# Layer 1 of a two-layer decoder: its wide products cut into 256-column products, with other places in SBUF and other orders

## Chip, cores and metric

One core of one Trainium2 chip. The metric is the device time of one execution in microseconds (us): 2316.28 us before the change, the median of two runs (2315.99 and 2316.57). A product here is one matmul instruction of TensorE: 128 rows of weights that stand still, and a number of columns that stream past them.

## What is computed

A decoder of two layers over 272 tokens (16 meta tokens and 256 of the input), model width 2048, 16 heads of 128, MLP width 8192, all in float32. Layer 0 (forgetting attention) computes all 272 tokens; layer 1 (stick-breaking attention) needs queries, output projection and MLP for the last 256 alone. Cut to what matters:

```
for layer in range(2):
    a = rms_norm(h, norm_attn[layer])
    if layer == 0:
        q, k, v, f = split(a @ fox_w_in)
        h = h + forgetting_attention(q, k, v, cumsum(log_sigmoid(f + b))) @ fox_w_o
    else:
        k, v = split(rms_norm(h, kv_norm) @ w_kv)
        h = h + stick_breaking_attention(a @ sb_w_q, k, v) @ sb_w_o
    h = h + square(relu(rms_norm(h, norm_mlp[layer]) @ w_up[layer])) @ w_down[layer]
return rms_norm(h, final_norm)[16:]
```

## The kernel before

Activations stay in SBUF with features on the partitions: `hT` holds 16 chunks of 128 features by 272 tokens. Every wide matrix product runs in `gemm_group` (L183): one call computes 512 output features, as four accumulators (`m` = 0 to 3, one PSUM bank each) that sum over 16 chunks of 128 inputs, in four blocks `kb` of four chunks `kc`. The groups are numbered `u` in program order: 1 to 12 are query, key and value of layer 0, 13 to 16 its output projection, 17 to 48 its MLP (for each quarter `f` of the width four up groups and four down groups), 49 to 52 the queries of layer 1, 53 to 60 its shared keys and values (which need all 272 tokens), 61 to 64 its output projection, and 65 to 96 its MLP in the same way.

To keep accuracy, each float32 operand is split into a high part, rounded to the fast float32r format, and a low part, the rest. Weights arrive by DMA on SP's queue in halves of a block (`raw`, 512 KB, L207), ScalarE writes `whi` (L218) and VectorE `wlo` (L219); four buffers of each let this run ahead. The activations ("rows" in the code, class `Split`, L118) hold high and low part of a chunk in 640 columns, at the column offsets in `ROWS` (L27). Three of the four partial products are added up: whi·hi, whi·lo and wlo·hi.

In layer 0 (and for keys and values) these are three products of 272 columns per chunk and accumulator. In layer 1 (`pairs=True`) hi and lo, 304 columns apart, are read as one operand of 2 x 256 columns:

```
gemm_matmul(accs[m], whi, sp.both[:, 4 * kb + kc], ...)       # 512 columns
gemm_matmul(accs[m][:, :n], wlo, sp.hi[:, 4 * kb + kc], ...)  # 256 columns
```

So whi·hi + wlo·hi stands in the left half of the bank and whi·lo in the right half, and VectorE (and ScalarE) add the halves when the bank is emptied: `total` (L259) for queries and up groups, two additions in `residual_add` (L255) for output projection and down groups. The very last chunk (group 96, `m` = 3, `apart`) runs as three products of 256 columns in one half. In layer 1 `wlo` is stored 16 columns further right than in layer 0.

The order of TensorE's instructions within and across groups is pinned as written (`gemm_matmul`, L175); other work, such as attention and norms, is placed between by a scheduler. A product's weights are loaded by an instruction of its own in the profile (LDWEIGHTS, engine PEld).

Of the kernel before, what the change touches and what calls it, by code (L numbers as in the profile page):

```python
# [12 lines left out]
ALU = mybir.AluOpType  # L13
AX = mybir.AxisListType

P = 128
D = 2048
NC = D // P
M = 16
# [7 lines left out]
ROWS = {0: (48, 368), M: (0, 304)}  # L27
# [6 lines left out]
def yoco_kernel(ctx: ExitStack, tc: tile.TileContext, hT_in, gains, b_f, w_f, w_qkv0, w_o0, w_up, w_dn,  # L34
# [83 lines left out]
    class Split:  # L118


        def __init__(self, label, t0):
# [3 lines left out]
            hi, lo = ROWS[t0]  # L125
# [3 lines left out]

            self.both = rows[:, :, :2 * d].rearrange("p c (i t) -> p c i t", i=2)[:, :, :, :n]  # L130
# [52 lines left out]
    def gemm_group(wblk, sp, t0, evac, before={}, after={}, load_x=None, pairs=False, apart=()):  # L183


# [7 lines left out]
        for kb in range(4):  # L193
# [31 lines left out]

            if load_x is not None and kb == 0:
                runs = [([kc], range(4)) for kc in range(4)]
            elif kb in (0, 3):
                runs = [(range(4), [m]) for m in range(4)]
            else:  # L230
                runs = [(range(2 * hf, 2 * hf + 2), range(4)) for hf in range(2)]
            pinned[0] = load_x is None
            for kcs, ms in runs:
                paired = [m for m in ms if pairs and m not in apart]
                single = [m for m in ms if m not in paired]
                for kc in kcs:
                    for m in paired:
                        gemm_matmul(accs[m], parts[kc // 2][0][:, kc % 2, m * P:(m + 1) * P], sp.both[:, 4 * kb + kc],
                                    start=kb == kc == 0, stop=False)
                for kc in kcs:  # L240
                    for m in paired:
                        gemm_matmul(accs[m][:, :n], parts[kc // 2][1][:, kc % 2, m * P:(m + 1) * P],
                                    sp.hi[:, 4 * kb + kc], start=False, stop=kb == kc == 3)
                for m in single:
                    for kc in kcs:
                        wh, wl = (w[:, kc % 2, m * P:(m + 1) * P] for w in parts[kc // 2])
                        hi, lo = sp.hi[:, 4 * kb + kc], sp.lo[:, 4 * kb + kc]
                        gemm_matmul(accs[m][:, :n], wh, hi, start=kb == kc == 0, stop=False)
                        gemm_matmul(accs[m][:, :n], wh, lo, start=False, stop=False)
                        gemm_matmul(accs[m][:, :n], wl, hi, start=False, stop=kb == kc == 3)  # L250
# [488 lines left out]
```

## Time and profile before

| | |
|---|---|
| median of the runs | 2316.28 us |
| profiled execution | 2316.17 us |
| its span, first to last instruction | 2314.5 us |
| granted TensorE clock, mean | 0.998 |
| HBM read | 407.29 MB, 177 GB/s over the span |
| mean busy share of VectorE, ScalarE | 58%, 46% |

"PE" is TensorE computing, "PEld" its weight loads, DVE VectorE, ACT ScalarE, POOL GpSimd, SP SyncE. A product's recorded duration (some 276 ns for 256 columns) is longer than the step from one start to the next, because products overlap in the array; the time a stretch takes comes from the starts, or from a stretch's length and its count of instructions. In the timeline a row merges neighbouring instructions of one kind: start, time covered, engine, line, operation, tiles, shape and count. In the grouped rows stand the busy time and the mean duration in ns, then the idle time ahead of them.

### The profile page before, as it was taken

To read this page: it belongs to the slowest core of one execution; us is meant where nothing else is said; L and a number is where in the kernel's file an instruction comes from. 1 tells how busy PE (TensorE), PEld (TensorE's weight loads), DVE (VectorE), ACT (ScalarE), POOL (GpSimd) and SP (SyncE) were. 2 spreads that over 40 slices of the span, in tenths; PEclk is the share of its full clock that TensorE was granted. 3 is DMA by queue.
4 is the path that set the end of the run, shared out by engine and by line. 5 is a ranking of instruction groups with operands and counts; after the bars stand their busy time and mean duration, and the time that the engine had idled before them with its cause. 6 is when DMAs were issued, how large, how long until landed. Compare 5 with 4: busy or idle time off the path is not lost.

```text
span 2314.5 us, 39954 instructions
## 1 busy us (share of the span) xinstructions
PE 2303.4 (100%) x16486; PEld 2183.1 (94%) x16486; DVE 1350.1 (58%) x1923; ACT 1064.1 (46%) x1477; POOL 40.8 (2%) x58
## 2 busy tenths in 40 slices
PE   9999999999999999999999999999999999999998
PEld 9999999999999999999998999988888888888887
DVE  7665555655454455445566555566665665665665
ACT  6434344543344344344445444455543543543553
POOL 1000000000000000000000000000000000000000
PEclk9999999999999999999999999999999999999999
DMA  6545445455555555555555444455556556556563
GB/s 233 169 155 170 166 163 170 168 187 174 181 170 186 179 175 181 173 184 175 182 178 200 157 146 146 146 169 196 193 188 199 185 190 200 185 191 199 183 200 128
DMA packets 116630, 412.00 MB, mean 178 GB/s; under 512 B 13264, under 2 KB 16736, under 8 KB 116448
## 3 DMA queue, kind: packets, MB, share of 16 engines
q1 hardware_dynamic: 114560, 406.29, 52.7%
q10 hardware_dynamic: 1888, 3.16, 0.4%
q8 instruction: 129, 2.11, 0.4%
q14 instruction: 53, 0.43, 0.1%
HBM read 407.29 MB, written 2.11 MB: 177 GB/s over the span
## 4 chain that ended last, share of the span: by engine, by line
PE 99%; DVE 0%; DMA 0%; ACT 0%; issue 0%; SPq 0%; DVEq 0%; ACTq 0%
PE acc L177 96%; PE ps L407 0%; PE pza L586 0%; PE pv L340 0%; PE po L469 0%; PE po L625 0%; PE pzb L587 0%; PE po L626 0%; PE po L470 0%; DMA g_sb<-gains 0%; PE po L627 0%; DVE ob L681 0%; PE pf L306 0%; PE pf L307 0%; PE pta L601 0%; PE pta L602 0%
## 5 line engine op out<-in xcount | busy, mean ns | idle before, releaser
L219 DVE TENSOR_TENSOR wlo<-raw,whi 128x1024 fp32r<-128x1024 f32 (+1 forms) x773 | 931.6, 1217 | 741.8 <-ACT whi L218 740.6
L218 ACT ACTIVATE whi<-raw 128x1024 fp32r<-128x1024 f32 (+1 forms) x773 | 799.1, 1050 | 948.0 <-PE acc L177 873.8
L177 PE MATMUL acc<-x_u,whi 128*128 128x272 f32 (+2 forms) x3088 | 647.9, 321 | 0.0
L177 PE MATMUL acc<-x_m,whi 128*128 128x272 f32 (+1 forms) x3072 | 646.2, 322 | 0.0
L177 PEld LDWEIGHTS acc<-x_u,whi 128*128 128x128 f32 x3088 | 499.5, 188 | 26.6
L177 PEld LDWEIGHTS acc<-x_m,whi 128*128 128x128 f32 x3072 | 497.5, 188 | 27.2
L177 PE MATMUL acc<-x_u,wlo 128*128 128x272 f32 (+1 forms) x2048 | 443.3, 281 | 0.0
L177 PE MATMUL acc<-x_m,wlo 128*128 128x272 f32 (+1 forms) x2048 | 441.0, 281 | 0.0
L177 PE MATMUL acc<-x_a,whi 128*128 128x272 f32 (+1 forms) x1792 | 360.6, 306 | 0.1
L177 PEld LDWEIGHTS acc<-x_u,wlo 128*128 128x128 f32 x2048 | 338.4, 188 | 15.8
L177 PEld LDWEIGHTS acc<-x_m,wlo 128*128 128x128 f32 x2048 | 337.5, 188 | 15.9
L177 PEld LDWEIGHTS acc<-x_a,whi 128*128 128x128 f32 x1792 | 284.2, 188 | 9.4 <-issue 0.7
L177 PE MATMUL acc<-x_a,wlo 128*128 128x272 f32 (+1 forms) x1024 | 254.0, 286 | 0.0
L177 PE MATMUL acc<-x_kv,whi 128*128 128x272 f32 x1024 | 194.1, 288 | 0.0
L177 PEld LDWEIGHTS acc<-x_a,wlo 128*128 128x128 f32 x1024 | 179.1, 188 | 5.3 <-DVE wlo L219 0.6
L177 PE MATMUL acc<-x_o,whi 128*128 128x272 f32 (+1 forms) x768 | 162.4, 322 | 0.0
L177 PEld LDWEIGHTS acc<-x_kv,whi 128*128 128x128 f32 x1024 | 160.6, 188 | 0.4
L177 PE MATMUL acc<-x_kv,wlo 128*128 128x272 f32 x512 | 147.3, 288 | 0.0
L257 DVE TENSOR_TENSOR hT<-acc,hT 128x256 f32<-128x256 f32 (+1 forms) x239 | 102.4, 428 | 70.5 <-PE acc L177 68.8
L177 PEld LDWEIGHTS acc<-x_o,whi 128*128 128x128 f32 x768 | 124.3, 188 | 6.7
L177 PE MATMUL acc<-x_o,wlo 128*128 128x272 f32 (+1 forms) x512 | 111.0, 282 | 0.0
L177 PEld LDWEIGHTS acc<-x_kv,wlo 128*128 128x128 f32 x512 | 96.5, 188 | 0.1
(226 smaller groups left out, 1040.0 us busy)
## 6 DMA issues: line engine op xcount, KB each, us to landing
raw<-w_up SPq DMA_DIRECT2D x256, 512.0 KB, 4.7
raw<-w_dn SPq DMA_DIRECT2D x256, 512.0 KB, 4.8
raw<-w_qkv SPq DMA_DIRECT2D x92, 512.0 KB, 4.3
raw<-w_o SPq DMA_DIRECT2D x64, 512.0 KB, 4.4
raw<-w_kv SPq DMA_DIRECT2D x64, 512.0 KB, 3.9
raw<-w_q SPq DMA_DIRECT2D x32, 512.0 KB, 4.8
fk<-f_dram ACTq DMA_DIRECT2D x4, 544.0 KB, 5.1
raw<-w_qkv SPq DMA_DIRECT2D x7, 256.0 KB, 4.6
```

What stands on the lines that cost most here:

```text
L177: ins = nc.tensor.matmul(*args, **kw).ins
L218: on_act = nc.scalar.activation(hp, src, AF.Copy)
L219: on_dve = nc.vector.tensor_tensor(out=lp, in0=src, in1=hp.bitcast(F32), op=ALU.subtract)
L257: nc.vector.tensor_tensor(out=hT[:, c, t0:], in0=a, in1=hT[:, c, t0:], op=ALU.add)
```

## The change

Layer 1 drops the 512-column products. `pairs`, `apart`, `Split.both` and `total` go; all groups issue three products per chunk and accumulator, in layer 1 of 256 columns each and all into the same accumulator columns. Emptying it takes one instruction less (two less in queries and up groups).

The places are now given by stage. `ROWS` is keyed by the rows' name, and low parts lie 320 columns after high parts everywhere; `columns_of_weights` shifts `whi` and `wlo` alike:

| layer-1 groups | rows start at column | weights start at column |
|---|---|---|
| queries 49-52, up 65-68, 73-76, 81-84, 89-92 | 0 | 16 |
| output projection 61-64 | 48 | 0 |
| down 69-72 | 48 | 0 |
| down 77-80 | 16 | 32 |
| down 85-88 | 48 | 32 |
| down 93-96 | 32 | 48 |

All other groups keep rows at 48 and weights at 0, and layer 0 keeps its order of products. A column is four bytes.

By group, `order` gives one of three nestings of products (chunk kc, accumulator m, pair), and in every fourth group the blocks `kb` 1 and 2 run as one stretch of four chunks:

```
+ROWS = {"a0": (48, 368), "kv": (48, 368), "o0": (48, 368), "m0": (48, 368), "u0_0": (48, 368),
+        "u0_1": (48, 368), "u0_2": (48, 368), "u0_3": (48, 368),
+        "a1": (0, 320), "o1": (48, 368), "m1": (0, 320), "u1_0": (48, 368), "u1_1": (16, 336),
+        "u1_2": (48, 368), "u1_3": (32, 352)}
+def columns_of_weights(u):
+    if u < 49 or 53 <= u <= 64:
+        return 0
+    f, g = divmod(u - 65, 8)
+    return 16 if u < 53 or g < 4 else (0, 32, 32, 48)[f]
+def order(u, kcs, ms, pairs):
+    way = (u - 1) % 4
+    if way == 0 or way == 3:
+        return [(kc, m, *pair) for pair in pairs for kc in kcs for m in ms]
+    if way == 1:
+        return ([(kc, m, *pair) for kc in kcs for m in ms for pair in pairs[:2]] +
+                [(kc, m, *pairs[2]) for kc in kcs for m in ms])
+    return [(kc, m, *pair) for kc in kcs for m in ms for pair in pairs]
...
-                whi, wlo = whi[:, :, :512], wlo[:, :, 16:528] if pairs else wlo[:, :, :512]
+                o = columns_of_weights(u)
+                whi, wlo = whi[:, :, o:o + 512], wlo[:, :, o:o + 512]
...
+            elif t0 and u % 4 == 0 and kb in (1, 2):
+                runs = [(range(4), range(4))]
...
             for kcs, ms in runs:
-                paired = [m for m in ms if pairs and m not in apart]
...
+                pairs = ((0, sp.hi), (0, sp.lo), (1, sp.hi))
+                if t0:
+                    products = order(u, kcs, ms, pairs)
+                else:
+                    products = [(kc, m, *pair) for m in ms for kc in kcs for pair in pairs]
+                left = {m: 3 * len(kcs) for m in ms}
+                for kc, m, part, x in products:
+                    first, left[m] = kb == kc == 0 and left[m] == 3 * len(kcs), left[m] - 1
+                    gemm_matmul(accs[m][:, :n], parts[kc // 2][part][:, kc % 2, m * P:(m + 1) * P], x[:, 4 * kb + kc],
+                                start=first, stop=kb == kc == 3 and left[m] == 0)
...
     def residual_add(c, acc, t0):
-        for a in acc:
-            nc.vector.tensor_tensor(out=hT[:, c, t0:], in0=a, in1=hT[:, c, t0:], op=ALU.add)
...
-        nc.scalar.copy(to, acc[1])
-        nc.vector.tensor_tensor(out=to, in0=acc[0], in1=to, op=ALU.add)
...
+        nc.vector.tensor_tensor(out=hT[:, c, t0:], in0=acc, in1=hT[:, c, t0:], op=ALU.add)
```

How instructions move on TensorE: the first half of block 1 in group 70 (a down group of layer 1; `x_u1_0` are its rows, `whi_70_1_0` the high weights of group 70, block 1, half 0). Before:

```order
L177 MATMUL acc_70_0_18477<-x_u1_0_17427,whi_70_1_0_18529 128x512
L177 MATMUL acc_70_1_18478<-x_u1_0_17427,whi_70_1_0_18529 128x512
L177 MATMUL acc_70_2_18479<-x_u1_0_17427,whi_70_1_0_18529 128x512
L177 MATMUL acc_70_3_18480<-x_u1_0_17427,whi_70_1_0_18529 128x512
...
L177 MATMUL acc_70_0_18477<-x_u1_0_17427,wlo_70_1_0_18530 128x256
L177 MATMUL acc_70_1_18478<-x_u1_0_17427,wlo_70_1_0_18530 128x256
L177 MATMUL acc_70_2_18479<-x_u1_0_17427,wlo_70_1_0_18530 128x256
L177 MATMUL acc_70_3_18480<-x_u1_0_17427,wlo_70_1_0_18530 128x256
```

and now:

```order
L198 MATMUL acc_70_0_19225<-x_u1_0_17891,whi_70_1_0_19293 128x256 x2
L198 MATMUL acc_70_1_19226<-x_u1_0_17891,whi_70_1_0_19293 128x256 x2
L198 MATMUL acc_70_2_19227<-x_u1_0_17891,whi_70_1_0_19293 128x256 x2
L198 MATMUL acc_70_3_19228<-x_u1_0_17891,whi_70_1_0_19293 128x256 x2
...
L198 MATMUL acc_70_0_19225<-x_u1_0_17891,wlo_70_1_0_19294 128x256
L198 MATMUL acc_70_1_19226<-x_u1_0_17891,wlo_70_1_0_19294 128x256
L198 MATMUL acc_70_2_19227<-x_u1_0_17891,wlo_70_1_0_19294 128x256
L198 MATMUL acc_70_3_19228<-x_u1_0_17891,wlo_70_1_0_19294 128x256
```

Each 512-column product has become two of 256 columns with the same weights, each with a weight load of its own. In group 71, the next, the same place reads:

```order
L198 MATMUL acc_71_0_19473<-x_u1_0_17891,whi_71_1_0_19541 128x256 x2
L198 MATMUL acc_71_0_19473<-x_u1_0_17891,wlo_71_1_0_19542 128x256
L198 MATMUL acc_71_1_19474<-x_u1_0_17891,whi_71_1_0_19541 128x256 x2
L198 MATMUL acc_71_1_19474<-x_u1_0_17891,wlo_71_1_0_19542 128x256
L198 MATMUL acc_71_2_19475<-x_u1_0_17891,whi_71_1_0_19541 128x256 x2
L198 MATMUL acc_71_2_19475<-x_u1_0_17891,wlo_71_1_0_19542 128x256
```

Here the three products of one accumulator and chunk follow one another, as in layer 0. On VectorE, emptying the up group 68 (`relu_1_0_12` is output chunk 12 of layer 1's first quarter) before:

```order
L264 TENSOR_TENSOR relu_1_0_12_18233<-acc_68_0_18077,relu_1_0_12_18233 128x256
L501 SCALAR_TENSOR_TENSOR relu_1_0_12_18233<-relu_1_0_12_18233,rstd_m1_17525 128x256
L264 TENSOR_TENSOR relu_1_0_13_18249<-acc_68_1_18078,relu_1_0_13_18249 128x256
L501 SCALAR_TENSOR_TENSOR relu_1_0_13_18249<-relu_1_0_13_18249,rstd_m1_17525 128x256
L505 TENSOR_TENSOR x_u1_0_17427<-u2_1_0_12_18234,x_u1_0_17427 128x256
```

and now:

```order
L506 SCALAR_TENSOR_TENSOR relu_1_0_12_18917<-acc_68_0_18709,rstd_m1_18021 128x256
L506 SCALAR_TENSOR_TENSOR relu_1_0_13_18935<-acc_68_1_18710,rstd_m1_18021 128x256
L510 TENSOR_TENSOR x_u1_0_17891<-u2_1_0_12_18918,x_u1_0_17891 128x256
L506 SCALAR_TENSOR_TENSOR relu_1_0_14_18953<-acc_68_2_18711,rstd_m1_18021 128x256
L510 TENSOR_TENSOR x_u1_0_17891<-u2_1_0_13_18936,x_u1_0_17891 128x256
```

The addition of the two halves is gone there, and ScalarE's copy ahead of it too. SP's queue of DMAs is the same in both, and so is TensorE's order up to group 49.

More of the change, by code (lines that the diff above doesn't have):

```diff
@@ L128, in __init__ @@
             self.hi, self.lo = rows[:, :, :n], rows[:, :, d:d + n]
-            self.both = rows[:, :, :2 * d].rearrange("p c (i t) -> p c i t", i=2)[:, :, :, :n]
     def split_chunk(sp, gi, c):
@@ L181, in gemm_matmul, with gemm_group @@
         queued[:] = [ins]
-    def gemm_group(wblk, sp, t0, evac, before={}, after={}, load_x=None, pairs=False, apart=()):
+    def gemm_group(wblk, sp, t0, evac, before={}, after={}, load_x=None):
         uid[0] += 1
@@ L233, in gemm_group @@
             for kcs, ms in runs:
-                paired = [m for m in ms if pairs and m not in apart]
[L235 to L250, printed above, removed]
+                pairs = ((0, sp.hi), (0, sp.lo), (1, sp.hi))
@@ L251, in gemm_group @@
                 if kb == 3:
                     for m in ms:
-                        evac(m, [accs[m][:, :n]] + ([accs[m][:, n:]] if m in paired else []))
+                        evac(m, accs[m][:, :n])
     def residual_add(c, acc, t0):
-        for a in acc:
-            nc.vector.tensor_tensor(out=hT[:, c, t0:], in0=a, in1=hT[:, c, t0:], op=ALU.add)
-    def total(acc, to):
-        if len(acc) == 1:
-            return acc[0]
-        nc.scalar.copy(to, acc[1])
-        nc.vector.tensor_tensor(out=to, in0=acc[0], in1=to, op=ALU.add)
-        return to
+        nc.vector.tensor_tensor(out=hT[:, c, t0:], in0=acc, in1=hT[:, c, t0:], op=ALU.add)
@@ L383, in yoco_kernel @@
             for m in range(4):
-                evac_q(m, [qT[:, m, :]])
+                evac_q(m, qT[:, m, :])
             forget_gates(box["rstd"])
@@ L484, in evac @@
                 norm.add(c)
-            gemm_group(w[g], ao, t0, evac, pairs=t0 == M)
+            gemm_group(w[g], ao, t0, evac)
         return xm, norm
@@ L500, in evac @@
                     u2 = tmp.tile([P, T], F32, tag="u2", name=f"u2_{layer}_{f}_{c}")
-                    nc.vector.scalar_tensor_tensor(out=r[:, t0:], in0=total(acc, r[:, t0:]), scalar=0.0, in1=box["r"][:, t0:],
+                    nc.vector.scalar_tensor_tensor(out=r[:, t0:], in0=acc, scalar=0.0, in1=box["r"][:, t0:],
                                                    op0=ALU.max, op1=ALU.mult)
@@ L506, in evac @@
                                             op=ALU.subtract)
-                gemm_group(w_up[layer, f, g], xm, t0, evac, {2: get_rstd} if f == g == 0 else {},
-                           pairs=t0 == M)
+                gemm_group(w_up[layer, f, g], xm, t0, evac, {2: get_rstd} if f == g == 0 else {})
             for g in range(4):
@@ L513, in evac @@
                         last_evac(4 * g + m)
-                gemm_group(w_dn[layer, f, g], u, t0, evac, pairs=t0 == M,
-                           apart=(3,) if layer == 1 and f == N_FF - 1 and g == 3 else ())
+                gemm_group(w_dn[layer, f, g], u, t0, evac)
     xm, norm_m = out_proj(w_o0, ao, 0, G_M0, "m0")
@@ L538, in evac_q1 @@
             q = qT1[g][:, m, :S]
-            nc.vector.scalar_tensor_tensor(out=q, in0=total(acc, q), scalar=QSCALE, in1=box["rstd"][:, M:],
+            nc.vector.scalar_tensor_tensor(out=q, in0=acc, scalar=QSCALE, in1=box["rstd"][:, M:],
                                            op0=ALU.mult, op1=ALU.mult)
@@ L545, in yoco_kernel @@
         gemm_group(w_q1[g], xq, M, evac_q1, {2: get_rstd1} if g == 0 else {},
-                   after={kb: (lambda kb=kb: split_c(kb)) for kb in range(4)} if g else {}, pairs=True)
+                   after={kb: (lambda kb=kb: split_c(kb)) for kb in range(4)} if g else {})
     ao = Split("o1", M)
```

9 lines of the change are left out of this document (4 added, 5 removed).

## Prediction

> **What bounds the kernel now.** I read the page first: the busy times and the chain that ended last.
>
> ```profile
> span 2314.5 us, 39954 instructions
> PE 2303.4 (100%) x16486; PEld 2183.1 (94%) x16486; DVE 1350.1 (58%) x1923; ACT 1064.1 (46%) x1477; POOL 40.8 (2%) x58
> PE 99%; DVE 0%; DMA 0%; ACT 0%; issue 0%; SPq 0%; DVEq 0%; ACTq 0%
> ```
>
> TensorE is busy through the whole span and is 99% of the chain. So the time is the number of products times the step from the start of one to the start of the next. Second view: busy times by stretch, one of layer 0 (groups 18 to 48) and one of layer 1 (groups 66 to 95).
>
> ```profile
> core 0: us, PE busy (x) PEld busy (x) DVE busy (x) ACT busy (x) POOL busy (x), PEclk, DMA share, GB/s
> 454.30:1188.40 734.10, 734.10 (x5954) 734.10 (x5953) 381.33 (x461) 314.51 (x400) 0.00 (x0) 1.00 0.53 178
> 1619.50:2278.70 659.20, 659.20 (x3843) 578.59 (x3841) 408.70 (x553) 319.71 (x447) 0.00 (x0) 1.00 0.59 192
> ```
>
> No gap stands in either, and the granted clock is 1.00. In layer 0 a 272-column product takes 734.10 / 5953 = 123.3 ns. In layer 1 the 30 groups hold 30 x 64 = 1920 pairs (one of 512 columns, one of 256), so a pair takes 659.20 / 1920 = 343.33 ns. Third view, the timeline, parts the pair; its first column is the start in us.
>
> ```profile
> 1756.83 2.00 PE L177 MATMUL acc<-x_u,whi 128*128 128x512 f32 x8
> 1758.67 1.07 PE L177 MATMUL acc<-x_u,wlo 128*128 128x256 f32 x8
> 1759.58 2.00 PE L177 MATMUL acc<-x_u,whi 128*128 128x512 f32 x8
> 1761.42 1.07 PE L177 MATMUL acc<-x_u,wlo 128*128 128x256 f32 x8
> ```
>
> Eight of 512 take 1.84 us, 230.0 ns each. What the pair leaves is 343.33 - 230.0 = 113.3 ns for the 256-column product, and 0.91 / 8 = 113.8 agrees within the rounding of the starts (1 ns each). A 256-column product thus takes a little less than half of the 512 one (115.0).
>
> One more price of 256 columns stands in the trace: the chunk that was set apart in the last group already runs three 256-column products per k chunk. This is the timeline of TensorE and its weight loads together.
>
> ```profile
> 2299.95 0.41 PE L177 MATMUL acc<-x_u,whi 128*128 128x256 f32 x2
> 2300.07 0.19 PEld L177 LDWEIGHTS acc<-x_u,wlo 128*128 128x128 f32 x1
> 2300.20 0.28 PE L177 MATMUL acc<-x_u,wlo 128*128 128x256 f32 x1
> 2300.20 0.31 PEld L177 LDWEIGHTS acc<-x_u,whi 128*128 128x128 f32 x2
> 2300.32 0.39 PE L177 MATMUL acc<-x_u,whi 128*128 128x256 f32 x2
> 2300.55 0.28 PE L177 MATMUL acc<-x_u,wlo 128*128 128x256 f32 x1
> 2300.66 0.40 PE L177 MATMUL acc<-x_u,whi 128*128 128x256 f32 x2
> 2300.90 0.28 PE L177 MATMUL acc<-x_u,wlo 128*128 128x256 f32 x1
> 2301.02 0.28 PE L177 MATMUL acc<-x_u,whi 128*128 128x256 f32 x1
> ```
>
> From 2299.95 to 2301.02 nine products take 1.07 us: 118.9 ns each, 5.6 ns over the 113.3 of the same width in the same group. The rows also show when a load is made: the load for the next product starts with the product before it (both at 2300.20). So rows and the next weights are read from SBUF at the same time, and the difference must lie in where they are read or in what order.
>
> **Where they lie.** The strides (640 columns of a rows chunk, 576 of a weight row, 128 of a slice) are multiples of 256 bytes, and the tiles begin on such multiples. So each product has one fixed distance: the byte at which its rows start, less the byte at which the next load's weights start, modulo 256. That this modulus is the one that counts is my choice; the strides keep no larger one fixed. In layer 0 rows start at columns 48 and 368 and weights at 0: distance 192. In layer 1 of before the wlo product has rows at 0 and wlo at column 16: 192 too. The products apart have 0, 128 and 0 (rows 0 or 304, weights 0 or 16). Cheap products have 192, the dear ones 0 and 128. In the change every layer-1 product has 192, since rows and slice move together (0 with 16, 48 with 0, 16 with 32, 32 with 48), except the down groups of the third quarter (85 to 88; rows 48, weights 32), which have 64.
>
> **The change part by part.** (1) Products. Layer 1 has 40 groups x 64 = 2560 places (chunk m by chunk k). 16 of them were already apart; the others are counted here, by form.
>
> ```profile
> L177 PE MATMUL acc<-x_m,whi 128*128 128x512 f32 x1024 | 266.9, 392 | 0.0
> L177 PE MATMUL acc<-x_u,whi 128*128 128x512 f32 x1008 | 262.9, 392 | 0.0
> L177 PE MATMUL acc<-x_o,whi 128*128 128x512 f32 x256 | 67.2, 393 | 0.0
> L177 PE MATMUL acc<-x_a,whi 128*128 128x512 f32 x256 | 66.9, 393 | 0.0
> ```
>
> That is 2544 pairs. Before: 2544 x 343.33 = 873.4 us, and 48 products apart at 118.9 = 5.7 us; together 879.1 us. After: 7680 products of 256 columns. Their price in these places isn't in the trace. Bounds: 118.9 above (the products apart), 113.3 as the cheapest row. I take 113.3, because distance 192 is what the 2560 wlo products and all of layer 0 have: 7680 x 0.1133 = 870.1 us, a gain of 9.0 us. The 4 x 192 = 768 products at distance 64 have no row: from nothing to 768 x 5.6 ns = 4.3 us; I take nothing, as 64 differs from 192 by 128 and from the dear places by an odd multiple of 64, and keep 4.3 for the range.
>
> (2) Orders. Within a group the three products now run in one of four orders. All have the same distance, and layer 0 runs its three products in one more order at the price above, so I put no cost on the order. In every fourth group two k blocks run as one stretch of 48, so the second half's weights are wanted after 16 products (1.8 us) and not after 24. The splits have the time; this row, of the waits, is ScalarE's largest in total, for buffers that TensorE still reads, so the weights are made early:
>
> ```profile
> ACT whi L218 <- PE acc L177: 873.8, 454, 4.4
> ```
>
> (3) Weight loads: 2544 more, each beside the product before it. In layer 0 they fill 734.10 of 734.10 us without slowing anything at 123.3 ns a product. At 113.3 ns the trace shows at most eight in a row. If they needed 118.9, this is the first rival.
>
> (4) Evacuation. One accumulator needs no adding up. The rows, by form, of layer 1 from the output projection on:
>
> ```profile
> L263 ACT COPY relu<-acc 128x256 f32<-128x256 f32 x64 | 23.7, 370 | 39.3 <-PE acc L177 39.3
> L264 DVE TENSOR_TENSOR relu<-acc,relu 128x256 f32<-128x256 f32 x64 | 27.1, 424 | 16.1 <-ACT relu L263 16.1
> L257 DVE TENSOR_TENSOR hT<-acc,hT 128x256 f32<-128x256 f32 x158 | 66.9, 423 | 30.9 <-PE acc L177 29.2
> ```
>
> With the query groups' 16, 80 copies (about 30 us), 80 additions (34 us) and half of the residual additions (79 x 0.423 = 33 us) go. All lie beside products, which have no gap, so I count nothing; without that cover they would be worth at most these sums. At the end nothing goes: the last chunk, set apart, has one addition already.
>
> ```profile
> 2302.01 0.42 DVE L257 TENSOR_TENSOR hT<-acc,hT 128x256 f32<-128x256 f32 x1 [0.98 <-PE acc L177]
> ```
>
> Nothing new is queued on SP or POOL, and no wait is added. Sum: the profiled execution's 2316.17 us (0.1 under the median of the runs shown) - 9.0 = **2307.2 us**; with the 4.3 of distance 64, 2311.5.
>
> The Trainium skill (TensorE: Matmul & The Clock Gate, "Back-to-back issue gap") gives the step of an isolated product as columns / 2.4 + 2.5 ns. That is 215.8 and 109.2 ns where the trace has 230.0 and 113.3, so the trace disagrees. By the rule a place goes from 325.0 to 327.5 ns, and the change would cost 2544 x 2.5 = 6.4 us; it speaks against the change.
>
> **The rivals.** *The price depends on the place itself, or on sustained loads* (the slower side). If only the places of the 20 groups whose rows still start at 0 (query, up) cost 113.3 and the other 20 cost 118.9, 20 x 192 x 5.6 ns = 21.5 us come back: 2316.2 - 9.0 + 21.5 = 2328.7 us. If all cost 118.9: 7680 x 0.1189 = 913.2, 34.1 more than 879.1: 2350.3 us. It decides from a mean of 879.1 / 7680 = 114.5 ns. For it: the only three-product stretch of this width does cost 118.9. Against: that stretch has the bad distances, and layer 0 keeps 192 and a steady 123.3.
>
> The Trainium skill (SBUF — State Buffer, "Who interferes with whom") holds that TensorE's two SBUF read ports, rows and weights, are independent and that it never waits on anyone. Then no place costs more than another. The 118.9 against 113.3 in one group disagrees.
>
> *Each instruction pays a fixed share.* From 256 to 272 columns the step grows by 123.3 - 113.3 = 10.0 ns, while 16 columns at 230.0 / 512 = 0.449 ns are 7.2; up to 2.8 ns could be such a share. Halving a 512 product pays it once more: 2544 x 2.8 = 7.1 us, less 0.2 for the products apart: 2323.1 us. Against it: the 256-column product costs less than half of the 512. By the Trainium skill's rule on the gap, above, it would be 2322.6.
>
> *A better place than any so far.* The floor would be the column time alone. The attention's 256-column products, at half the column rate, show it: two take 0.43 us.
>
> ```profile
> 1309.97 0.59 PE L586 MATMUL pza<-qT,kT 128*128 128x256 f32 x2
> 1310.40 0.41 PE L587 MATMUL pzb<-qT,kT 128*128 128x144 f32 x2
> ```
>
> That is 215 ns each, so 107.5 at the full rate, an estimate. Half way there, 110.4 ns, gives 847.9 us: 2285.0 us. Nothing in the trace runs this cheaply.
>
> **How the numbers follow.** Forecast 0.55 (own range 2305 to 2312), place or loads 0.28 (2313 to 2350), fixed share 0.11, better place 0.06. The range runs from 2302 to 2334: below lies the better place, above it the upper part of the first rival, some 0.14 together. Two per cent is 46 us, about what a measurement of this kernel can tell from no change. Faster by that needs a mean under 108.4 ns (0.02), slower one over 120.5 (0.03), so within it 0.95.
>
> **What would show it.** Right: groups 66 to 84 at 192 x 113.3 ns = 21.75 us each instead of 21.97, four orders alike, no gap on TensorE. Distance counts: groups 85 to 88 alone longer (up to 22.8 us). The place counts: down groups longer than up groups. A fixed share: every group alike at about 22.15. Wrong altogether: idle time on TensorE in layer 1, or layer 0 no longer at 123.3 ns.

## The result, and the profile after

The change makes the kernel slower by 0.7%: 2331.39 us, the median of two runs (2331.07 and 2331.71), against 2316.28; the ratio is 1.0066 [1.0045, 1.0088]. The forecast was 2307.2, so the sign was wrong, though 2331.4 lies inside the range (2302 to 2334). The profiled execution took 2331.71 us, 15.5 more than that of before.

The page of the changed kernel, busy times and chain:

```profile
span 2329.6 us, 44815 instructions
PE 2318.3 (100%) x19030; PEld 2305.3 (99%) x19030; DVE 1287.6 (55%) x1764; ACT 1038.5 (45%) x1397; POOL 39.4 (2%) x58
PE 99%; DVE 0%; DMA 0%; ACT 0%; issue 0%; SPq 0%; DVEq 0%; ACTq 0%
```

TensorE is still 99% of the chain, so no new wait took the time. It has 2544 products more, as foreseen (19030 - 16486), and VectorE is 62.5 us less busy. The loss has to lie in the step. These are stretches of TensorE in the changed kernel; the first column is the stretch in us, then its length, the busy time and the count of products, which is 2 or 3 over the number begun, since a product that overlaps the edge counts too.

```profile
1620.50:1685.80 65.30, 65.30 (x579) 1.00 0.59 194
1708.40:1776.20 67.80, 67.80 (x578) 1.00 0.57 186
1798.80:1866.70 67.90, 67.90 (x579) 1.00 0.56 186
1889.30:1957.10 67.80, 67.80 (x578) 1.00 0.57 186
1978.90:2044.20 65.30, 65.30 (x579) 1.00 0.60 194
2066.80:2134.60 67.80, 67.80 (x578) 1.00 0.58 187
2157.30:2225.10 67.80, 67.80 (x579) 1.00 0.57 186
454.30:1187.80 733.50, 733.50 (x5950) 1.00 0.55 178
```

Each row but the last is the last three groups of an MLP stage, 3 x 192 = 576 products: groups 66 to 68, 70 to 72, 74 to 76, 78 to 80, 82 to 84, 86 to 88, 90 to 92. There are two lengths and nothing between. 65.30 / 576 = 113.4 ns, and 67.80 / 576 = 117.7 ns; from the starts of the single products the two steps are 113.33 and 117.78 ns. I call them the fast and the slow step (groups 86 to 88, at distance 64, are taken up again below): a group takes 21.76 or 22.61 us, 0.853 us apart. The last row is layer 0, still 123.3 ns. The clock is 1.00 in all of them, and nowhere is TensorE idle.

Rows 1, 3, 5 and 7 are the four up stages. They read the same tile of rows, at the same place (rows 0, weights 16), in the same four orders, and yet the first and the third run fast, the second and the fourth slow. So neither place nor order, as the prediction understood them, sets the price. The timeline shows the step in a row of products, first in group 67, then in group 70:

```profile
1640.88 1.07 PE L198 MATMUL acc<-x_m,whi 128*128 128x256 f32 x8
1641.79 0.62 PE L198 MATMUL acc<-x_m,wlo 128*128 128x256 f32 x4
```
```profile
1726.75 1.11 PE L198 MATMUL acc<-x_u,whi 128*128 128x256 f32 x8
1727.69 0.63 PE L198 MATMUL acc<-x_u,wlo 128*128 128x256 f32 x4
```

Eight products take 0.91 us in the one and 0.94 in the other. The single starts are 113 or 114 ns apart in the one and 117 or 118 in the other: each product is some 4.4 ns longer, not one in eight. And the step changes in the middle of a group. In group 65 of the changed kernel, two small products of the norm come between blocks 1 and 2:

```profile
1606.33 2.05 PE L198 MATMUL acc<-x_m,whi 128*128 128x256 f32 x16
1608.21 1.10 PE L198 MATMUL acc<-x_m,wlo 128*128 128x256 f32 x8
1609.16 0.59 PE L179 MATMUL pms_m<-ssq_m,mean_w 128*128 128x256 f32 x2
1609.40 2.18 PE L198 MATMUL acc<-x_m,whi 128*128 128x256 f32 x16
1611.42 1.07 PE L198 MATMUL acc<-x_m,wlo 128*128 128x256 f32 x8
1612.32 1.86 PE L198 MATMUL acc<-x_m,whi 128*128 128x256 f32 x15
```

Before them 16 products take 1608.21 - 1606.33 = 1.88 us (117.5 ns each), after them eight take 1612.32 - 1611.42 = 0.90 us (112.5). (The 16 between them hold the end of the norm's products, too: 306 ns pass from the start of the first to that of the second.) From there to the end of group 68 the step stays fast. By groups, fast are 49 (blocks 0, 1), 61 (from block 1) to 64, 65 (blocks 2, 3) to 68, and 81 to 84; slow are the other half of 49, 50 to 52, the first half of 65, 69 to 80 and 85 to 96. That is 28 groups, 28 x 0.853 = 23.9 us. The forecast gained 9.0 us on the kernel before; with 23.9 us on top, the change loses 14.9, and the spans differ by 15.1. The whole loss is in these 28 groups.

### The profile page after: what moved, and what is told of

It is laid out like the page before. It is cut to its first block, busy times and chain, and to the rows that moved or that the text cites. A ratio compares the mean times of both kernels' runs of the same rounds, so it can differ in the third digit from the quotient of the medians.

```text
span 2329.6 us, 44815 instructions
## 1 busy us (share of the span) xinstructions
PE 2318.3 (100%) x19030; PEld 2305.3 (99%) x19030; DVE 1287.6 (55%) x1764; ACT 1038.5 (45%) x1397; POOL 39.4 (2%) x58
## 4 chain that ended last, share of the span: by engine, by line
PE 99%; DMA 0%; DVE 0%; ACT 0%; issue 0%; SPq 0%; DVEq 0%; ACTq 0%
PE acc L198 95%; PE ps L412 0%; DMA raw<-w_qkv 0%; PE pza L589 0%; PE pv L345 0%; PE po L474 0%; PE po L628 0%; PE po L629 0%; PE pzb L590 0%; PE po L475 0%; PE po L630 0%; DVE ob L684 0%; PE pf L312 0%; PE pf L311 0%; PE pta L604 0%; PE pta L605 0%
## 5 line engine op out<-in xcount | busy, mean ns | idle before, releaser
L198 PE MATMUL acc<-x_u,whi 128*128 128x272 f32 (+1 forms) x4096 | 672.8, 284 | 0.0
L198 PE MATMUL acc<-x_m,whi 128*128 128x272 f32 (+1 forms) x4096 | 668.2, 283 | 0.0
L198 PEld LDWEIGHTS acc<-x_u,whi 128*128 128x128 f32 x4096 | 588.4, 189 | 0.0
L198 PEld LDWEIGHTS acc<-x_m,whi 128*128 128x128 f32 x4096 | 584.7, 188 | 0.1
L198 PE MATMUL acc<-x_u,wlo 128*128 128x272 f32 (+1 forms) x2048 | 477.8, 284 | 0.0
L198 PE MATMUL acc<-x_m,wlo 128*128 128x272 f32 (+1 forms) x2048 | 475.7, 283 | 0.0
L198 PEld LDWEIGHTS acc<-x_a,whi 128*128 128x128 f32 x2048 | 306.5, 189 | 3.0 <-issue 0.7
L198 PE MATMUL acc<-x_a,wlo 128*128 128x272 f32 (+1 forms) x1024 | 262.9, 287 | 0.0
L198 PEld LDWEIGHTS acc<-x_o,whi 128*128 128x128 f32 x1024 | 145.5, 188 | 0.1
L270 DVE TENSOR_TENSOR hT<-acc,hT 128x272 f32<-128x272 f32 (+1 forms) x160 | 69.0, 431 | 87.2 <-PE acc L198 86.5
```

Of the source, the lines that this page charges most:

```text
L198: ins = nc.tensor.matmul(*args, **kw).ins
L270: nc.vector.tensor_tensor(out=hT[:, c, t0:], in0=acc, in1=hT[:, c, t0:], op=ALU.add)
```

## The experiments

Theory, from the trace: in layer 1 of the change a 256-column product has two steady steps in the same place. Which one holds is kept from product to product and changes only where something else comes between: another width, a norm, a change of place between stages. Rivals: the price belongs to the place (rival one of the prediction, with another table of places), to the order of a group, or to the load. "Extra product" below means one more product into a bank that nobody reads, so extra work and the same output. Each run is a kernel of its own, with runs of the kernel before on the same chip (2315.2 to 2316.4). All but e5 and e11 were run once; which groups are fast or slow is read from the one trace of each.

**One place for all of layer 1** (e1_uniform):

```
-        "a1": (0, 320), "o1": (48, 368), "m1": (0, 320), "u1_0": (48, 368), "u1_1": (16, 336),
-        "u1_2": (48, 368), "u1_3": (32, 352)}
+        "a1": (0, 320), "o1": (0, 320), "m1": (0, 320), "u1_0": (0, 320), "u1_1": (0, 320),
+        "u1_2": (0, 320), "u1_3": (0, 320)}
...
-    if u < 49 or 53 <= u <= 64:
+    if u < 49 or 53 <= u <= 60:
...
-    return 16 if u < 53 or g < 4 else (0, 32, 32, 48)[f]
+    return 16
```

> Edit: all layer-1 stages with rows at column 0 and weights at column 16; orders as in the change. Theory 1 (a phase that persists): a stretch of 256-column products runs at a step of 113.3 or of 117.8 ns, set when the stream enters the stretch or is disturbed (a stage whose place differs from the last one, a pause for a norm) and kept from there; so with one place no group from the middle of 65 to 96 differs from its neighbours: either all at 21.76 us (about 2311 us in all) or all at 22.61 us (about 2338 us). Theory 2 (each stage has its own price, by its tiles or by what runs beside it): quarters go on alternating between 21.76 and 22.61 us, about 2331 us.

Measured 2338.14 us. Both steps stand in one place: groups 62 to 64, and 70 to 72, of this kernel:

```profile
1533.10:1598.40 65.30, 65.30 (x579) 1.00 0.60 194
1711.40:1779.30 67.90, 67.90 (x579) 1.00 0.58 186
```

The slow step begins at block 2 of group 65, right behind the norm's two products, and then holds to the end. Its timeline there, to be set beside the one above:

```profile
1606.53 1.98 PE L197 MATMUL acc<-x_m,whi 128*128 128x256 f32 x16
1608.35 1.07 PE L197 MATMUL acc<-x_m,wlo 128*128 128x256 f32 x8
1609.26 0.59 PE L178 MATMUL pms_m<-ssq_m,mean_w 128*128 128x256 f32 x2
1609.50 2.23 PE L197 MATMUL acc<-x_m,whi 128*128 128x256 f32 x16
1611.57 1.10 PE L197 MATMUL acc<-x_m,wlo 128*128 128x256 f32 x8
1612.51 2.05 PE L197 MATMUL acc<-x_m,whi 128*128 128x256 f32 x16
```

Here 16 products take 1.82 us before the norm and eight take 0.94 after it: the same two products that turned slow into fast in the change turn fast into slow here. Nothing changes at any stage boundary of this kernel. So a price of the place by itself can't part the fast groups from the slow ones here.

**One order for all groups** (e2_one_order):

```
-    way = (u - 1) % 4
+    way = 0
...
-            elif t0 and u % 4 == 0 and kb in (1, 2):
-                runs = [(range(4), range(4))]
```

> Edit: all layer-1 groups in the first of the four orders, no stretch of four chunks; places as in the change. Theory 1 (phase) and theory 2 (stage): the same groups are slow as in the change (50 to 52, 69 to 80, 85 to 96 at 22.61 us), 2331 us within 1.5. Theory 3 (the order decides, the slow step being started by one of the orders): other groups are slow or none, 2308 to 2340 us.

Measured 2330.30 us, with the same groups fast and slow as in the change. It is 15.1 us over the kernel before that ran with it (2315.22), as the change is over its own, so the orders and the longer stretch are worth nothing that can be seen.

**The change with an extra product of 512 columns** (e3_wide_512) **or of 256** (e4_extra_256) ahead of each layer-1 stage and after two norms:

```
+            self.both = rows[:, :, :2 * d].rearrange("p c (i t) -> p c i t", i=2)[:, :, :, :n]
...
+            if t0 and (kb == 0 and u % 4 == 1 or kb == 2 and u in (49, 65)):
+                sync = patt.tile([P, 512], F32, tag="patt", name=f"sync_{u}_{kb}")
+                gemm_matmul(sync[:, :2 * n], parts[0][0][:, 0, :P], sp.both[:, 4 * kb], start=True, stop=True)
```

This is e3; in e4 the operand is `sp.hi[:, 4 * kb]`. The extra products of the runs below read `both` as well, the two halves as one operand.

> Edit: the change, plus one extra product of 512 columns (hi and lo together, into a bank that nobody reads) ahead of each layer-1 stage and after the two norms, 12 in all, 0.23 us each. Theory 1 with the wide product as what sets the phase (a weight load has slack beside it, as in the kernel before): all groups at 21.76 us, about 2331.4 - 23.9 + 2.8 = 2310.3 us. Theory 2 (stage), or a wide product that sets nothing: slow groups as in the change, about 2334.2 us.

> Edit: as the run with the extra 512-column products, but the 12 extra products have 256 columns, 0.11 us each. Theory 1 with the width as what matters: some stages stay slow, about 2333 us (2320 to 2340, since a disturbance may turn a stage either way). If any break in the stream sets the fast step: all groups at 21.76 us, about 2309 us. Theory 2 (stage): slow groups as in the change, 2332.8 us.

Measured 2319.63 and 2334.15 us. With 512 columns, all of 69 to 84 and 89 to 96 are fast, and only 61 to 64 and 85 to 88 slow; stretches of groups 62-64, 70-72 and 86-88:

```profile
1533.60:1601.50 67.90, 67.90 (x579) 1.00 0.56 187
1711.50:1776.70 65.20, 65.20 (x578) 1.00 0.60 195
2061.40:2129.20 67.80, 67.80 (x578) 1.00 0.57 186
```

With 256 columns the pattern is another one again: 65-68 slow, 69-72 fast, 89-92 fast. Twelve products beside 7680 change the step of some 28 groups (e3) and some 12 (e4), so the step hangs on what goes before. But neither number was met: both kernels also lose 4 to 5 us between groups 53 and 62 (258.4 and 259.0 us from start to start, against 254.3), where group 61 holds less of attention's work than in the change (22.61 and 21.78 us, against 27.66) and the groups ahead of it more.

**One place, with three extra products** at block 2 of groups 49, 61 and 65, of 512 columns (e5_uniform_512, three rounds) or of 272 (e6_uniform_272):

```
+            if t0 and (kb == 2 and u in (49, 61, 65)):
+                sync = patt.tile([P, 512], F32, tag="patt", name=f"sync_{u}_{kb}")
+                gemm_matmul(sync[:, :272], parts[0][0][:, 0, :P], sp.both[:, 4 * kb, :, :136], start=True, stop=True)
```

> Edit: the run with one place for all layer-1 stages, plus three extra products of 512 columns (0.23 us each): after each of the two norms (group 49 and 65, before block 2) and after the last attention work (group 61, before block 2). Theory 1 (the phase persists; a wide product with 192 bytes of distance sets the fast one): all layer-1 groups from there at 21.76 us, 8.1 us under the kernel before (2308.2 against 2316.3). If the phase is lost again at a change of stage or buffer even with one place: some stages at 22.61 us, 2311 to 2335 us. If the extra product sets nothing: 2338 us as without it.

> Edit: as the run with three extra 512-column products, but of 2 x 136 = 272 columns. Theory 1a (any product that outlasts a weight load sets the fast phase, as layer 0 runs at one steady step with 272 columns): as that run, 8.5 us under the kernel before. Theory 1b (much slack is needed): at least one of the three stretches stays at 117.8 ns, up to 2338 us.

512 columns: 2338.52 us (2337.96 to 2340.06), ratio 1.0099 [1.0081, 1.0117]. The idea that a wide product sets the fast step fell: 50 to 52 became fast, 62 to 64 slow, 66 to 96 stayed slow as in e1. 272 columns: 2307.48 us, every layer-1 group fast.

**Distances** (e7_distances): up stages in the one place, the four down stages at distance 0, 128, 32 and 64, with an extra 512 ahead of each MLP stage from group 69 on and at block 2 of groups 49, 61 and 65.

```
-        "a1": (0, 320), "o1": (48, 368), "m1": (0, 320), "u1_0": (48, 368), "u1_1": (16, 336),
-        "u1_2": (48, 368), "u1_3": (32, 352)}
+        "a1": (0, 320), "o1": (0, 320), "m1": (0, 320), "u1_0": (48, 368), "u1_1": (0, 320),
+        "u1_2": (0, 320), "u1_3": (48, 368)}
...
-    if u < 49 or 53 <= u <= 64:
+    if u < 49 or 53 <= u <= 60:
...
-    return 16 if u < 53 or g < 4 else (0, 32, 32, 48)[f]
+    return 16 if u < 65 or g < 4 else (48, 32, 56, 32)[f]
...
+            if t0 and (kb == 0 and u > 65 and u % 4 == 1 or kb == 2 and u in (49, 61, 65)):
...
```

> Edit: up groups, queries and output projection at rows 0, weights 16 (distance 192 bytes); the four down stages at distances 0 (rows 48, weights 48), 128 (rows 0, weights 32), 32 (rows 0, weights 56) and 64 (rows 48, weights 32); a 512-column product ahead of every MLP stage and where the three-product run has them. If the distance decides which phase a wide product leaves behind: the up groups fast (21.76 us), down groups with 64 slow (22.61) and those with 0, 128 and 32 slow too if 192 alone is good; about 2322 us if all 16 are slow. If a wide product alone decides: all groups fast, about 2310 us.

Measured 2342.09 us. The down groups 70-72, 78-80, 86-88 and 94-96, in this order:

```profile
1712.80:1781.90 69.10, 69.10 (x579) 1.00 0.57 183
1895.60:1963.90 68.30, 68.30 (x578) 1.00 0.57 185
2077.30:2144.40 67.10, 67.10 (x577) 1.00 0.59 188
2258.00:2325.80 67.80, 67.80 (x579) 1.00 0.43 140
```

From start to start, over whole groups, they are 120.0, 118.7, 116.7 and 117.8 ns: distances 0 and 128 cost more than either step of distance 192, and 32 lies between them. So the place has a part in the price; it just doesn't decide between 113.3 and 117.8. Each distance ran in one place and was entered once, so whether those places have a second step isn't known. All up groups ran at the slow step here, and neither sum (2322, 2310) was met.

**Only the place, with the pairs of before** (e8_place_only): the kernel before, rows at 0 and 320, both weights at 16.

```
-ROWS = {0: (48, 368), M: (0, 304)}
+ROWS = {0: (48, 368), M: (0, 320)}
...
-                whi, wlo = whi[:, :, :512], wlo[:, :, 16:528] if pairs else wlo[:, :, :512]
+                o = 16 if pairs else 0
+                whi, wlo = whi[:, :, o:o + 512], wlo[:, :, o:o + 512]
```

> Edit: the kernel before with the change's place for layer 1 (rows 0 and 320, weights whi and wlo at 16), its 512 and 256-column pairs kept. Tells the place from the cut. If places have a price of their own without long stretches of 256 columns: a step of the 512 product other than 230.0 ns, and a time off 2316 by more than 1.5 us either way. If only the cut brings the two phases: 2316 within 1.5, pairs at 343.3 ns.

Measured 2324.58 us. Three groups (66 to 68) take 66.60 us, so a pair takes 66.60 / 192 = 346.9 ns; by single groups (22.19 us) it is 346.7, against 343.3 before.

**Which width sets which step** (e9_widths_slow, e10_widths_fast): the one place, and ahead of the seven later MLP stages one extra product each, its width falling from 512 to 256. The second kernel differs only in an extra 272 at block 2 of group 65, which makes it enter group 69 fast.

```
+            if t0 and (kb == 0 and u > 65 and u % 4 == 1):
+                sync = patt.tile([P, 512], F32, tag="patt", name=f"sync_{u}_{kb}")
+                width = {69: 256, 73: 192, 77: 160, 81: 144, 85: 136, 89: 130, 93: 128}.get(u, 136)
+                gemm_matmul(sync[:, :2 * width], parts[0][0][:, 0, :P], sp.both[:, 4 * kb, :, :width], start=True, stop=True)
```

> Every layer-1 product in the one place (rows 0 and 320, weights 16), no extra product before group 69, and ahead of the seven MLP stages after the first one extra product each, into a bank that nobody reads, of a falling number of columns: 512 (group 69), 384 (73), 320 (77), 288 (81), 272 (85), 260 (89), 256 (93). In the uniform place without extras the slow step began at kb 2 of group 65 and stayed to the end, so this run enters group 69 in the slow step (117.8 ns a product, 22.61 us a group). Theory (an extra product that is longer than the load beside it by only a little sets the fast step, a far longer one does not): groups 85 to 92 at 21.76 us, the stage after 512 still at 22.61, the widths between decide where the line runs; if all from 73 on is fast about 2338.1 - 24 x 0.853 + 0.8 = 2318.5, if only 85 to 96 about 2338.1 - 12 x 0.853 + 0.8 = 2328.7. Rival (any extra product just turns the step to the other one): stages alternate, 69-72 fast, 73-76 slow, 77-80 fast, and so on, about 2338.1 - 16 x 0.853 + 0.8 = 2325.3.

> The run of falling widths once more, with one extra product of 272 columns at kb 2 of group 65 added, after which the groups were at 21.76 us before, so that this run enters group 69 in the fast step (113.3 ns). Theory (the width decides which step follows, whatever stood before): each stage from 69 on takes the same step as in the run that enters in the slow step. Rival (any extra product turns the step): each stage takes the opposite step of the run that enters slow, 69-72 at 22.61 us. Third (the wide ones leave the step that stands): 69-72 at 21.76 here and at 22.61 there. All groups fast from 65 on gives about 2338.1 - 30 x 0.853 + 0.9 = 2313.4, strict turning about 2338.1 - 18 x 0.853 = 2323.

Measured 2318.88 and 2318.69 us. Of the two sums expected for e9, the one for "all from 73 on fast" (2318.5) came out by accident: 77 to 80 were slow, and 69 to 72 fast. By stage, the extra product and what followed:

| ahead of group | columns | e9: before, after | e10: before, after |
|---|---|---|---|
| 69 | 512 | slow, fast | fast, slow |
| 73 | 384 | fast, fast | slow, fast |
| 77 | 320 | fast, slow | fast, slow |
| 81 | 288 | slow, fast | slow, fast |
| 85, 89, 93 | 272, 260, 256 | fast, fast | fast, fast |

None of the three simple theories holds for every width: here 512 turned the step, 384 and 288 were followed by the fast one, 320 by the slow one. The last row tells nothing, since the groups were fast before and after.

**The version without the slow step, timed** (e11_best, the kernel of e6, five rounds):

> The kernel of one place with three extra products of 272 columns (groups 49, 61 and 65, kb 2), which ran once at 2307.48 against 2316.09 for the kernel before, timed in rounds. Theory: the fast step in all of the 40 groups is held by the program and not by chance, so 2307.5 within half a us in each run, ratio about 0.9963. Rival (the step after a 272-column product falls either way from run to run): runs spread over 2307 to 2338, in steps of about 3.4 us for each stage that falls to the slow step.

Measured 2308.43 us (2307.77 to 2309.57), ratio 0.9966 [0.9952, 0.9979]. Groups 66 to 95 of it, in one stretch:

```profile
1617.90:2270.70 652.80, 652.80 (x5763) 1.00 0.60 194
```

30 x 192 = 5760 products in 652.80 us are 113.33 ns each, without a break. It beats both kernels, the one before by 0.3%. The half us expected for each run was missed (the longest is 2.1 over 2307.5), but no run reached the next count of slow groups (3.4 us for a stage), so the step doesn't seem to fall at random.

**The change's own places with 272-column products** (e12_places_272), ahead of all stages but that of 61, and at block 2 of 49, 61 and 65:

```
+            if t0 and (kb == 0 and u % 4 == 1 and u != 61 or kb == 2 and u in (49, 61, 65)):
+                sync = patt.tile([P, 512], F32, tag="patt", name=f"sync_{u}_{kb}")
+                gemm_matmul(sync[:, :272], parts[0][0][:, 0, :P], sp.both[:, 4 * kb, :, :136], start=True, stop=True)
```

> The change with its own places by stage and orders, and one extra product of 272 columns at the first of each layer-1 stage (49, and 65 to 93) and at kb 2 of groups 49, 61 and 65. Theory (a 272-column product sets the fast step in any place at a distance of 192 bytes): all stages at 21.76 us, only 85-88 (distance 64) at 22.61 as after the 512-column products: 2331.4 - 23.9 + 12 x 0.123 + 4 x 0.853 = 2312.4, and 2309.0 if 85-88 are fast too. Rival (what the 272-column product does hangs on the step that stood before, so it turns some stages to slow): some stages beside 85-88 at 22.61, each 3.4 us more, up to about 2333.

Measured 2315.99 us: 3.6 over the first number, because 89 to 92 were slow beside 85 to 88 (4 x 0.853 = 3.4 us more). In four different places at distance 192 the groups were fast. These twelve products are all that differs from the change, and they make it 15.4 us shorter. At distance 64 the groups took 22.61 us again, after another width.

**Does 512 turn, do 272 and 320 set?** (e13_turns, e14_sets): as e9, with other widths, first those of e13, then those of e14.

```
...
+                width = {69: 256, 73: 256, 77: 256, 81: 256, 85: 136, 89: 136, 93: 256}.get(u, 136)
```
```
...
+                width = {69: 136, 73: 160, 77: 160, 81: 192, 85: 160, 89: 136, 93: 144}.get(u, 136)
```

> One place for all layer-1 products, entered in the slow step at group 69; extra products into a bank nobody reads ahead of groups 69, 73, 77, 81 (512 columns each), 85 and 89 (272 each) and 93 (512). Theory (in this place a 512-column product turns the step to the other one, a 272-column product sets the fast one): 69-72 fast, 73-76 slow, 77-80 fast, 81-84 slow, 85-92 fast, 93-96 slow; slow groups from the start 49 kb 2 to 52, 65 kb 2 to 68, and 12 more, so 2308.4 + (3.5 + 3.5 + 12) x 0.853 + 1.4 = 2326.0. Rival (what follows a 512-column product is not tied to the step before): not that alternation; with all four of the 512 stages fast 2308.4 + 7 x 0.853 + 1.4 = 2315.8, with all four slow 2308.4 + 23 x 0.853 + 1.4 = 2329.4. If a 272-column product leaves the slow step as it is, 85-92 are slow too: 6.8 us more.

> The same place and entry in the slow step; extra products ahead of group 69 of 272 columns, 73 of 320, 77 of 320, 81 of 384, 85 of 320, 89 of 272, 93 of 288. Theory (320 columns set the slow step, 272, 288 and 384 the fast one, whatever stood before): 69-72 fast, 73-80 slow, 81-84 fast, 85-88 slow, 89-96 fast: 2308.4 + (7 + 12) x 0.853 + 0.9 = 2325.5. Rival (320 turns the step): 77-80 fast, 3.4 us less. Second rival (272 columns leave the step that stood): 69-72 and 89-92 slow, up to 6.8 us more.

Measured 2325.12 and 2324.42 us, and stage by stage what the theory said. The stretches of e13 are groups 70-72, 74-76, 78-80, 82-84, 86-88 and 94-96, after extra products of 512, 512, 512, 512, 272 and 512 columns:

```profile
1710.00:1775.20 65.20, 65.20 (x578) 1.00 0.58 194
1798.10:1865.90 67.80, 67.80 (x578) 1.00 0.58 187
1887.90:1953.20 65.30, 65.30 (x579) 1.00 0.60 194
1976.00:2043.90 67.90, 67.90 (x579) 1.00 0.57 187
2065.80:2131.10 65.30, 65.30 (x579) 1.00 0.59 193
...
2241.10:2308.90 67.80, 67.80 (x580) 1.00 0.43 140
```

Fast, slow, fast, slow after 512, each time the other one; 272 made slow fast. Of e14, groups 70-72, 74-76, 78-80 and 82-84, after 272, 320, 320 and 384:

```profile
1709.80:1775.10 65.30, 65.30 (x578) 1.00 0.59 194
1797.90:1865.70 67.80, 67.80 (x578) 1.00 0.56 187
1888.50:1956.30 67.80, 67.80 (x578) 1.00 0.57 186
1978.30:2043.50 65.20, 65.20 (x578) 1.00 0.60 194
```

320 is followed by the slow step from either side, so it sets and doesn't turn. In the one place, what an extra product leaves was the same for its width each time, and for 512 hung on the step before it.

**Does the place decide anything alone?** (e15_pairs_turned: e8 with extras of 272, 384 and 512 columns; e16_distance_64: e12 with 288, 384, 320 and 512 ahead of 85, 86, 87 and 88, and 272 in group 90.)

```
+            if pairs and kb == 2 and u in (49, 61, 65, 69, 73):
...
+                w = {69: 192, 73: 256}.get(u, 136)
```
```
-            if t0 and (kb == 0 and u % 4 == 1 and u != 61 or kb == 2 and u in (49, 61, 65)):
+            if t0 and (kb == 0 and (u % 4 == 1 and u != 61 or 86 <= u <= 88) or kb == 2 and u in (49, 61, 65, 90)):
...
+                w = {85: 144, 86: 192, 87: 160, 88: 256}.get(u, 136)
```

> The pairs of before in the moved places (rows 0 and 320, both weights at 16; 2324.58 us, 22.19 us a group), with an extra product into a bank nobody reads at kb 2 of groups 49, 61, 65 (272 columns), 69 (384) and 73 (512). Theory (the 3.4 ns that a pair costs more there belong to the place, a pair has one step in one place): every group stays at 22.19 us, about 2324.6 + 0.8 = 2325.4. Rival (the pair has two steps as well and the moved place only happened to run in the slow one): groups after at least one of the extra products at 21.97 us, 2316.1 + 0.8 = 2316.9 if all are.

> The change with its own places and a 272-column product at each stage start (2315.99 us, groups 85 to 92 at 22.61, all other layer-1 groups at 21.76), but ahead of groups 85, 86, 87 and 88 (rows 48, weights 32, distance 64) one product of 288, 384, 320 and 512 columns, and one more of 272 at kb 2 of group 90. Theory (at distance 64 only the slow step stands, whatever goes before; in 89-92 both can stand): 85 to 88 at 22.61 each, 90 kb 2 to 92 at the fast step: 2316.0 + 0.7 - 2.5 x 0.853 = 2314.6; if 90 to 92 stay slow 2316.7. Rival (85 to 88 have both steps and fell to the slow one each time): at least one of 85 to 88 at 21.76, each 0.85 less, down to 2311.

Measured 2325.15 and 2315.31 us. The pairs in the moved place, groups 70-72 (behind 384 columns) and 74-76 (behind 512) of e15:

```profile
1710.10:1776.70 66.60, 66.60 (x387) 58.10 (x386) 38.45 (x48) 24.89 (x25) 0.00 (x0) 1.00 0.58 190
1799.10:1865.70 66.60, 66.60 (x387) 58.11 (x386) 42.61 (x61) 37.19 (x61) 0.00 (x0) 1.00 0.57 190
```

Every group from 66 on takes the 22.19 us of e8, but for the extra products, so in this place none of the three widths brought a second step for the pair, and the 3.4 ns are the place's. Of e16, groups 86 to 88 (with their three extra products) and 91, 92:

```profile
2055.20:2123.60 68.40, 68.40 (x581) 1.00 0.58 184
2168.70:2212.20 43.50, 43.50 (x386) 1.00 0.60 195
```

Less some 0.5 us for the three, the first stretch is 67.9 / 576 = 117.8 ns. After products of 272 to 512 columns in five widths (and in the change after none) distance 64 has run at 117.8 and never at 113.3. It has the length of the slow step, but it is not the same thing: in the slow step of every trace here products are recorded at 281 ns, at distance 64 mostly at 279 or 280. 91 and 92, with the place of the up groups, take 43.50 / 384 = 113.3 ns, fast again from block 2 of group 90 on: the 272-column product there made slow fast.

**The account.** With n the groups at 22.61 us in each trace (a half where the step changes at block 2), those at distance 64 included, I take 2308 us for the kernel without any (e6 and e11 less their extra products are 2307.1 and 2308.0), and the rest is 0.853 us a group and what the extra products take (0.1 us for each of 272 columns, 0.2 for 512):

| kernel | n | worked out | measured |
|---|---|---|---|
| the change | 28 | 2331.9 | 2331.4 |
| e1, one place | 35 | 2337.9 | 2338.1 |
| e5, 512 columns three times | 35.5 | 2339.0 | 2338.5 |
| e2, one order | 28 | 2331.9 | 2330.3 |
| e9, widths | 11 | 2318.4 | 2318.9 |
| e10, widths | 11.5 | 2319.0 | 2318.7 |
| e12, places and 272 | 8 | 2316.3 | 2316.0 |
| e13, turns | 19 | 2325.6 | 2325.1 |
| e14, sets | 19 | 2325.2 | 2324.4 |
| e16, distance 64 | 5.5 | 2314.8 | 2315.3 |

e3 and e4 lose time elsewhere as well, and e7 has other prices.

## Why the prediction was wrong, step by step

- **What bounds the kernel** was right: TensorE has no gap before or after, and the difference is a step times a count.
- **The step that failed** is in part (1): "I take 113.3, because distance 192 is what the 2560 wlo products and all of layer 0 have". It takes the price of a product as a function of its place. The 256-column products of before never ran next to one of their own width for long: they come in rows of four or eight between products of 512 columns. (Nor do all 2560 have distance 192: the last of each row has a load of `whi` behind it, at column 0, which is distance 0, and 16 are in the chunk set apart.) In the change 28 of 40 groups ran at 117.8 ns, 24 of them at distance 192, so layer 1 took about 870.1 + 23.9 = 894.0 us, a mean of 116.4 ns, past the 114.5 that the prediction named as the point where the gain is gone. Both steps stand at the same distance, in the same tiles, in the same order (the up stages; e1).
- **Distance 64** was costed at nothing with 4.3 us kept for the range. It cost 4 x 0.853 = 3.4 us, and it is, as far as the runs go, a price of the place: no width ahead of it made it faster. The bound was sound, the argument by odd multiples of 64 was not.
- **Distance 0 and 128 dear** was right in sign: 120.0 and 118.7 ns in e7. But the distance is no full account of the place: a pair at rows 0 and 320 and weights 16 costs 346.7 ns, whichever of three widths goes before (e8, e15), and the sum had no term for this, since the change has no pairs.
- **Orders** at nothing: right within the 1 us that single runs differ by (e2). **Sustained loads** at nothing: right; 5760 loads in a row beside products at 113.33 ns (e11). **Evacuation** at nothing: right, since TensorE had no gap to give back. **Nothing new waits**: right.
- **The first rival** gave 2328.7 us for 20 groups at 118.9 ns, near the measured time, by a mechanism that did not occur: it priced the down groups by their place, and there were 28 groups at 117.8, up and down. That the range held the measured time is this rival's doing, and luck.
- **Fixed share** and **a better place** fell: in e6 and e11 all 40 groups of layer 1 run at 113.3 ns but for products beside a norm or attention, with no share more, and no run has a lower step over a whole group.
- **What would show it** worked halfway. "groups 85 to 88 alone longer" and "down groups longer than up groups" were both false, and a third outcome that it didn't list, equal groups at two prices, was what the stretches showed.

The Trainium skill's rule on the step of an isolated product (TensorE: Matmul & The Clock Gate, "Back-to-back issue gap") gives 109.2 ns for 256 columns; the steps over whole stretches here are 113.33 and 117.78. By its sum the change would cost 6.4 us; it cost 15.1, for another reason. That the two read ports are independent (SBUF — State Buffer, "Who interferes with whom") doesn't agree, in the prediction's reading that no place then costs more than another, with e7, where four places of rows and weights gave 116.7 to 120.0 ns for the same products.

What stays open: what in TensorE keeps the step. The records of the weight loads do part the two, in every trace: in the slow step exactly every third load is recorded at 191 to 193 ns, nearly always 192, and the others at 187 or 188 (192 of 575 loads in groups 70 to 72 of the change), in the fast step none of 576 is over 188 (groups 66 to 68). At distance 64 none of 576 is either (groups 86 to 88), and at distance 0 in e7 all but one are at 192. So the slow step is a rhythm of three products in which loads and products stand otherwise than in the fast one, and the stage at distance 64 shares its length alone. Why such a rhythm lasts, and why 320 columns lead to it and 288 and 384 to the other, wasn't derived.

Nor do the rules of the one place hold beyond it. In e3, where the places change from stage to stage, 512 columns ahead of 73, 77 and 81 left the fast step as it was. 272 columns ahead of 89 left 117.8 in e12, behind the stage at distance 64; inside the stage (block 2 of group 90, e16) they made it fast. And the norm's two products of group 65 turned slow into fast in the change, but with one more product of 256 columns right behind them (e4) the step stayed slow.

## What to carry to other kernels

A price read from products that stand among others of another width is a price for that mixture. Before a kernel is rebuilt on it, look for a long uniform stretch of that product, or count it as unknown by more than the rows' own bounds. When groups with identical instructions fall into two lengths, compare them pairwise by place and order first; if these don't separate them, look at what ran last before the length changed, and try one odd product there. Here one of 272 columns at three points of the program was worth 30.7 us to the kernel of one place (e1 against e6), and 0.3% against the kernel before.

## What the runs showed of the hardware

- A 256-column product with its own weight load has two steady steps at distance 192, 113.33 and 117.78 ns; each was seen in all four places of the change, and each was held for some 700 us in one place (e11, e1). In the slow one every third load is recorded some 4 ns longer. 272 columns were seen at one step (123.3, layer 0), and a pair of 512 and 256 columns at one in each of two places (343.3, and 346.7 behind three widths).
- One extra product changes it (one place, rows 0, weights 16): 512 columns turned the step, seven times in seven in e9, e10 and e13; behind 272, 288 and 384 it was the fast one, behind 320 the slow one. Two 256-column products of a norm turned it in both directions, but not in e4, with a third behind them.
- At other distances the same product cost up to 6.7 ns more than 113.3: 120.0 at distance 0, 118.7 at 128, 117.8 at 64, 116.7 at 32 (e7; one place each, entered once but for 64).
